# Out projection of a decoder step: seven block products in place of eight

## The chip, the cores and the metric

The kernel runs on one core of a Trainium2 chip. The metric is device microseconds (us) for one execution of the whole program. The kernel before takes 1403.93 us (median of 3 runs, 1402.64 to 1404.23). Its engines are called here as the profile calls them: PE (TensorE: matmuls; PEld are its weight loads), DVE (VectorE), ACT (ScalarE), POOL (GpSimd) and SP (the queue from which nearly all DMA transfers are issued). Each engine works through its own queue in order; semaphores make one wait for another. SBUF is the on-chip memory of 128 partitions, PSUM the small memory into which PE accumulates.

## The reference

One decoder layer runs over 1024 prompt tokens and 64 sample tokens (8 sequences of 8). Of its work the change touches the third line:

```python
branch_a = a_mix @ w_pa ;  branch_b = attn @ w_pb
mixed = sigmoid(g_a) * branch_a + sigmoid(g_b) * branch_b      # 1088 tokens x 1024
h = x + mixed @ w_o                                            # w_o: 1024 x 1024
y = h + relu(rmsnorm(h) @ w_up)**2 @ w_down                    # D_FF = 4096
```

Everything is float32. A few other outputs (pooling state, key/value windows) leave the chip on the side.

## The kernel before, in words

**Layout.** Activations are kept transposed: a row tile is 128 channels (partitions) by tokens. The 1088 tokens (`TOK`) stand in two halves of `H` = 544, called j = 0 and 1. A matrix of 1024 channels is eight row tiles k = 0..7. A float32 factor is split into a high part (an ACT copy to fp32r, L116) and a low part (DVE: source minus high, L117); a product takes three passes, high x high, high x low, low x high (`PASSES`). `split` issues the pair L116, L117. Split weights lie in one large tile, `places`; split activations in `act[0]` (high) and `act[1]` (low).

**Stages around the change.** First come the gate products (`pg`), which already use seven block products where eight would be the plain way; then the branch units (`pab`, `ab_unit`), sixteen of them, 36 matmuls each, first the eight of token half 0 and then the eight of half 1 in the row-block order d = 2, 0, 1, 3. A unit loads its two sigmoid gates (`gg0`, `gg1`), and its `post` multiplies them into the two branch products and adds them (DVE, L1643 and L1644); the mixed row is then split into `act`. Next is the out projection (`ph`), a loop over token half j, weight panel d (four panels of 256 output channels) and m = 0, 1 (128 channels each): one output row tile of 544 tokens is two `gemm` calls (264 and 280 tokens), each of 8 k-tiles x 3 passes, so 48 matmuls to a row and 768 in all. Both token halves read the whole of `w_o`, so it is loaded and split twice (32 loads of 256 KB, `raw_o`). After a row's matmuls, DVE adds the input x (L1751 in half 0; L1754 in half 1, where ACT has copied x into place, L1752); the row is stored to DRAM (`h_d`), squared on ACT (L1760) and summed for the norm (L1761). While half 1 is being multiplied, the norm of half 0 is finished: `norm_sums` (a small PE product `rth` at L1708, two DVE rows, a power on POOL), `norm_spread` (a DVE row `dg`, then the PE product `bc`, L1721), the eight `normed` rows on DVE (L1724), and `first_half`, which splits them into `act` and stores them. Last come the up projection (`pz`, seven block products again) and the down projection (`pd`). The sums for the second token half's norm are taken after the first `pz` product.

**What sets the order.** The order of PE's instructions is the order of the program text: PE works through products one after the other. Each queued piece has a `prep` (weights are split, sums formed; issued up to three pieces ahead), an `mm` (its matmuls) and a `post`; `run` steps through them. What ACT, DVE, POOL and SP do is put in order by a scheduler when the program is built, and from then on each of them keeps that order. PSUM holds four accumulator tiles for these products (`xtile`, used in turn), so a product that opens a new tile waits until the tile of four openings earlier has been read. `rr` gives buffers in turn in the same way: a load into a buffer waits for the last reader of what was there. POOL's queue also issues copies of the sample key/value windows to the outputs (`out_kv_sample`).

Of the kernel before, what the change touches and what calls it, by code (L numbers as in the profile page):

```python
# [7 lines left out]
F32 = mybir.dt.float32  # L8
# [7 lines left out]
P = 128  # L16
# [21 lines left out]
def decoder_step(ctx, tc, i, o):  # L38
# [183 lines left out]
    pg_d = dp.tile([8, P, H], F32, name="pg_d")  # L222
    ts_d = dp.tile([4, P, 4, H], F32, name="ts_d")
# [1340 lines left out]
    abs_, abq = right("ab0")  # L1564
    for n in T:
        B[n if n == "22" else f"T{n}"] = version(*T[n])
    abt = [abq.tile([P, 7 * 576 + H], F32R, name="ab0"), None]
    gg_first = {(m, x): abq.tile([P, H], F32, name=f"ggf{m}{x}") for m in range(2) for x in range(2)}

# [27 lines left out]
    AB_AT = (3072, 6144, 0, 9216)  # L1597
# [6 lines left out]
    gabs = gab = None  # L1604
    held_back = []

    def turn_to_ab():
        nonlocal gabs, gab
        gls.close()
        gqs.close()  # L1610
        gabs, gab = left("gab")
        abt[1] = gab.tile([P, 7 * 576 + H], F32R, name="ab1")

    def ab_unit(j, d, m):
        g = {}

        def load():
            for x in range(2):
                g[x] = gg_first[m, x] if j + d == 0 else rr(gab, [P, H], F32, name=f"gg{x}_{j}{d}{m}", tag=f"gg{x}", bufs=4)
                behind_pe(dma(g[x], g_d[4 * x + d, m][:, half(j)]))  # L1620
# [20 lines left out]
        def post():  # L1641
            for x in range(2):
                v_.tensor_tensor(two(g[x]), two(g[x]), xs_of(g["x"][x], ab_cut(j, x)), op=ALU.mult)  # L1643
            v_.tensor_tensor(g[0], g[0], g[1], op=ALU.add)  # L1644
            k = 2 * d + m
            out = lambda: split(*(act[s][k][:, half(j)] for s in range(2)), g[0])
# [5 lines left out]
            else:  # L1652
                out()

# [16 lines left out]
    run()  # L1671
    gabs.close()
    abs_.close()
    rows_s.close()


    wq = pool("wq", reuse_waits="tile")
    raws = {}
# [13 lines left out]
    y1s, y1p = right("y1")  # L1692
    nps, np_p = right("hn")
    hqs, hq_p = right("hq")
    y0s, y0p = right("y0")
    fours = [[pool_.tile([P, 4, H], F32, name=f"y{j}_{a}") for a in range(2)] for j, pool_ in enumerate((y0p, y1p))]
    y = [[fours[j][k // 4][:, k % 4] for k in range(KD)] for j in range(2)]
    sqa = [np_p.tile([P, H], F32, name=f"sqa{j}") for j in range(2)]
    hms = np_p.tile([P, 10], F32, name="hms")
    hr = np_p.tile([P, 10], F32, name="hr")  # L1700
    v_.memset(hr, 0.0)
# [28 lines left out]
    todo = []  # L1730
    place[0] += (2 - (place[0] + 8)) % 3
    for j in range(2):
        for d in range(4):
            wt = by_k(panel(i["w_o"][d], f"o{j}{d}"))
            if j == 0:
# [502 lines left out]
```

## Time and profile before

| what | before |
|---|---|
| runs | 1403.93 us median (1402.64 to 1404.23) |
| the profiled execution | 1407.21 us, its span 1405.4 us |
| PE busy | 1394.7 us (99% of the span) |
| DVE busy | 958.3 us (68%) |
| ACT busy | 753.7 us (54%) |
| POOL busy | 255.3 us (18%) |
| gate products end, branch products start | about 547 us |
| out projection (`ph`), first and last matmul | 634.7 to 732.3 us, 768 matmuls |

The profiled execution is 3.3 us above the median of the runs, which is within what single executions differ by, and 1.8 us above its own span. The busy shares are means over stages that have different limits: POOL's 18% lies almost all in the first 400 us, and between the branch products and the up projection it does next to nothing. DVE's 68% is not even either: in the branch products it has stretches with no gap at all. What counts for a change in one stage is which wait ends last in that stage.

### The profile page before, as it was taken

The page shows a single profiled execution, that of the slowest core. Times are in us where ns is not written, and L with a number is a line of the kernel's source. Part 1 is how long each engine was busy: PE and PEld are TensorE (multiplying, and loading weights), DVE is VectorE, ACT ScalarE, POOL GpSimd, SP SyncE. Part 2 cuts the span into 40 slices and gives each one's busy share as a digit, 9 for nine tenths or more (in the row PEclk, how much of TensorE's full clock was granted, in tenths as well). Part 3 has the DMA queues.
Part 4 walks back from the last instruction along what each step waited for, and adds up shares of the span by engine and source line. Part 5 has one row for each costly group of instructions (what it writes and reads, how often), then busy time and mean ns, then how long its engine had stood idle before and what let it go on. Part 6 is the DMA issues. An engine that isn't in the chain of part 4 may idle for free.

```text
span 1405.4 us, 29330 instructions
## 1 busy us (share of the span) xinstructions
PE 1394.7 (99%) x11101; PEld 1344.4 (96%) x11101; DVE 958.3 (68%) x1714; ACT 753.7 (54%) x1778; POOL 255.3 (18%) x362
## 2 busy tenths in 40 slices
PE   9999999999999999999999999999999999999998
PEld 8988987887999999999999999999999999999998
DVE  7778744776776767876468678665665686664566
ACT  8556775787765323563336455454554544444443
POOL 0744355676500000000000000000000000000100
PEclk9999999999999999999999999999999999999999
DMA  6455876755477777975468668856758988787674
GB/s 215 132 178 169 252 234 211 223 137 141 123 255 228 247 233 239 314 237 176 133 200 285 227 221 275 267 195 213 251 191 270 332 275 261 230 245 231 206 257 169
DMA packets 180701, 311.96 MB, mean 222 GB/s; under 512 B 26824, under 2 KB 82574, under 8 KB 178511
## 3 DMA queue, kind: packets, MB, share of 16 engines
q1 hardware_dynamic: 174926, 258.04, 57.0%
q0 software_dynamic: 5632, 52.04, 11.5%
q8 instruction: 87, 1.43, 0.4%
q14 instruction: 56, 0.45, 0.1%
HBM read 239.94 MB, written 122.12 MB: 258 GB/s over the span
## 4 chain that ended last, share of the span: by engine, by line
PE 70%; DMA 2%; DVE 1%; ACT 0%; issue 0%; SPq 0%; DVEq 0%; ACTq 0%
PE pz L1318 23%; PE pd L2096 23%; PE pg L1318 11%; PE ph L200 7%; PE pab L1318 4%; DMA raw_ab<-in_w_ab_dram 1%; DMA raw_d<-in_w_down_dram 0%; ACT places L116 0%; PE pog0b L723 0%; PE sg0b L690 0%; PE tpg0b L709 0%; PE pk L200 0%; PE pv L200 0%; SPq L127 0%; DVE places L117 0%
## 5 line engine op out<-in xcount | busy, mean ns | idle before, releaser
L2096 PE MATMUL pd<-places 128*128 128x272 f32 x2688 | 332.0, 287 | 0.7 <-DVE t L1960 0.7
L2096 PEld LDWEIGHTS pd<-places 128*128 128x128 f32 x2688 | 331.6, 188 | 0.9 <-DVE t L1960 0.9
L116 ACT ACTIVATE places<-raw_d 128x544 fp32r<-128x544 f32 (+1 forms) x176 | 110.5, 646 | 161.9 <-DMA raw_d<-z_d 51.3
L2136 POOL DMA_DIRECT2D out_kv_sample_dram<-in_cache_kv_dram x96 | 47.0, 490 | 793.1 <-ACT places L116 583.9
L117 DVE TENSOR_TENSOR places<-raw_d,places 128x544 fp32r<-128x544 f32 (+1 forms) x176 | 122.5, 711 | 91.7 <-ACT places L116 90.7
L1318 PE MATMUL pz<-act,places 128*128 128x280 f32 (+1 forms) x1080 | 139.4, 287 | 0.0
L1318 PEld LDWEIGHTS pz<-act,places 128*128 128x128 f32 x1080 | 135.9, 188 | 0.0
L200 PE MATMUL ph<-act,places 128*128 128x280 f32 (+1 forms) x768 | 96.6, 287 | 0.0
L200 PEld LDWEIGHTS ph<-act,places 128*128 128x128 f32 x768 | 96.0, 188 | 0.1
L1318 PE MATMUL pg<-act,places 128*128 128x264 f32 (+1 forms) x576 | 75.6, 288 | 0.0
L1318 PEld LDWEIGHTS pg<-act,places 128*128 128x128 f32 x576 | 72.6, 188 | 0.6 <-issue 0.3
L1318 PE MATMUL pz<-places,apart 128*128 128x264 f32 (+1 forms) x528 | 67.9, 287 | 0.0
L1318 PEld LDWEIGHTS pz<-places,apart 128*128 128x128 f32 x528 | 66.6, 188 | 0.0
L200 PE MATMUL pqk<-places,act 128*128 128x512 f32 x240 | 62.2, 410 | 0.0
L1318 PE MATMUL pz<-act,apart 128*128 128x264 f32 (+1 forms) x456 | 59.1, 287 | 0.0
L1318 PEld LDWEIGHTS pz<-act,apart 128*128 128x128 f32 x456 | 57.5, 188 | 0.1
L200 PEld LDWEIGHTS pqk<-places,act 128*128 128x128 f32 x240 | 45.8, 196 | 10.1
L874 POOL TENSOR_TENSOR pck<-pck,qs 128x256 f32<-128x256 f32 x64 | 49.9, 812 | 21.6 <-DMA pck<-own_d 7.6
L652 POOL TENSOR_TENSOR mr<-ms,mhalf 128x4 f32<-128x4 f32 (+2 forms) x39 | 51.3, 1317 | 2.9 <-POOL ms L651 0.2
L329 PE MATMUL a<-act,places 128*128 128x384 f32 (+1 forms) x288 | 50.9, 334 | 1.0 <-ACT act L307 0.9
L1318 PE MATMUL pab<-ab,places 128*128 128x264 f32 (+1 forms) x384 | 50.6, 287 | 0.2 <-DVE gg L1643 0.2
L329 PEld LDWEIGHTS a<-act,places 128*128 128x128 f32 x288 | 47.9, 188 | 2.9 <-ACT act L307 1.8
(436 smaller groups left out, 2811.7 us busy)
## 6 DMA issues: line engine op xcount, KB each, us to landing
out_kv_sample_dram<-in_cache_kv_dram POOLq DMA_DIRECT2D x72, 480.0 KB, 4.8
raw_d<-z_d SPq DMA_DIRECT2D x112, 272.0 KB, 4.3
z_d<-t SPq DMA_DIRECT2D x80, 272.0 KB, 4.0
raw_d<-in_w_down_dram SPq DMA_DIRECT2D x80, 256.0 KB, 3.8
raw_u<-in_w_up_dram SPq DMA_DIRECT2D x64, 256.0 KB, 4.0
raw_qkv<-in_w_in_dram SPq DMA_DIRECT2D x36, 256.0 KB, 3.8
own_d<-in_cache_kv_dram POOLq DMA_DIRECT2D x32, 256.0 KB, 3.4
pck<-own_d SPq DMA_DIRECT2D x16, 512.0 KB, 4.7
```

The lines of the kernel that those rows point to most:

```text
L116: ins = s_.activation(dst_hi, src, AF.Copy)
L117: v_.tensor_tensor(dst_lo, src, dst_hi.bitcast(F32), op=ALU.subtract)
L200: last_mm[0] = t_.matmul(out, lhs(a, k), rhs(b, k), start=(j == 0), stop=(j == len(terms) - 1))
L329: last_mm[0] = t_.matmul(pts[m][:, :n], wt[:, a, kk, m * P:(m + 1) * P], act4[b][kk][:, :, part4(c)], start=(p == 0 and kk == 0), stop=(p ...
L652: last_norm[0] = g_.tensor_tensor(r[:n, :H], ms[:n, :H], mhalf[:n, :H], op=ALU.pow)
L874: ins = g_.tensor_tensor(out, *others, op=ALU.mult)
L1318: last_mm[0] = t_.matmul(out[c], lhs(*term), rhs(*term, c), start=(first and n == 0), stop=(n == len(terms) - 1), skip_group_check=not first)
L2096: last_mm[0] = t_.matmul(outs(chain[t], Q)[c], A[:, a, t * P:(t + 1) * P], Z[:, b, c], start=(fresh and f == 0 and n == 0), stop=(f == NG ...
L2136: ins = g_.dma_start(d, a)
```

## The change

The out projection is rewritten as seven block products. Tokens are cut in two halves (column blocks of the mixed matrix), channels in two halves (k = 0..3 and 4..7), and the output channels of a panel f in two (m = 0, 1), so a panel is a 2 x 2 by 2 x 2 block product. With weight blocks A11, A12, A21, A22 and mixed blocks B11 .. B22, the seven products use sums of weights and sums of mixed rows (`sum1`, `sum2`, `sum3`), and the outputs are sums of products. A block product is 4 k-tiles x 3 passes x 2 column halves = 24 matmuls; four panels by seven products are 28 products or 672 matmuls. They run in the order

- 1 and 2 of panels 0 and 1, then of 2 and 3 (positions 0 to 7; these need only the token half that is finished first),
- 6, 7, 4 of panels 0 and 1 in turn (positions 8 to 13), then of panels 2 and 3 (14 to 19),
- 5 and 3 of panels 0 and 1 (20 to 23), then of panels 2 and 3 (24 to 27).

Beside that:

- The mixed rows of token half 0 are also stored to DRAM (`m_d`, eight stores of 272 KB) and eight times loaded back: into `early`, `gg1_back` and the not yet used half of `y`.
- New sums of mixed rows: sum1 and sum2 on DVE, sum3 and `y[1] -= t2f` on POOL. Their splits go to `places` (t_spot) and to `act`.
- New sums of weights for each panel (`sums_6`): A11 -= A21 and S2 = A22 - A11 on DVE, A21 += A22 and A12 -= S2 on POOL.
- x is added differently: `post2` adds it to one row on DVE (from PSUM) and to three more on POOL (strided reads of x by token). The x tiles are now eight loads of 544 KB into three buffers, where they were four loads of 1088 KB into two. A copy of product 1 out of PSUM is made on ACT.
- POOL so gets 28 tensor_tensor instructions of 128x544 or 128x512 in this place: 4 sum3, 4 `y[1] -= t2f`, 12 in `post2`, 8 sums of weights.
- `w_o` is loaded once, as eight quarters of 256 KB for products 1 and 2 and then as whole panels into the raw buffers (sixteen loads of 256 KB).
- The norm of token half 0 moves: `norm_sums(0)` between the column halves of position 21, `norm_spread(0)` and four `normed` after 22, four more after 23, `first_half` spread over 23 to 26.

The core of the diff:

```diff
+    def sum1(k):
+        b11 = mixed[0, k]
+        v_.tensor_tensor(b11, mixed[1, k], b11, op=ALU.subtract)
+        split(*(act[s][k][:, half(1)] for s in range(2)), b11)
+    def sum3(k):
+        g_.tensor_tensor(mixed[1, k], mixed[1, 4 + k], mixed[1, k], op=ALU.subtract)
+    def sum2(k):
+        t = t2f.setdefault(k, mixed[0, k])
+        v_.tensor_tensor(t, mixed[1, 4 + k], mixed[0, k], op=ALU.subtract)
+        split(*(t_spot(2, k, s) for s in range(2)), t)
...
+    def open_out():
...
+        for k in range(4):
+            dma(y[1][4 + k], m_d[4 + k])
+        for k in (2, 3):
+            sum1(k)
+            sum3(k)
+            sum2(k)
+        for k in range(4):
+            g_.tensor_tensor(y[1][4 + k], y[1][4 + k], t2f[k], op=ALU.subtract)
...
+    def load_x(f, m):
+        xr[f, m] = rr(hq_p, [P, TOK], F32, name=f"xr{f}_{m}", tag="xr", bufs=3)
+        dma(xr[f, m], i["xT"][:, 2 * f + m])
...
+    def put_out(src, key):
+        put_at[0] += 1
+        return put_weights(weights_at(1152 * (put_at[0] % 3)), src, [], key)
+    def load_out(f):
+        raws[f] = [raw_tile(f"o{f}_{a}") for a in range(2)]
+        for n in range(0, 2048, 512):
+            behind_pe(dma(raws[f][n // 1024][:, n % 1024:n % 1024 + 512], i["w_o"][f][:, n:n + 512]))
+    def put_plane(n, src):
+        hi, lo = (act_t[s][:, 4 + n, 8:520].rearrange("p (a b n) -> p a b n", a=2, b=2) for s in range(2))
+        split(hi, lo, src.rearrange("p (a b) n -> p a b n", b=2))
...
+        def post2():
+            v_.tensor_tensor(two(y[0][2 * f]), xs_of(q["x"]), by_token(xr[f, 0], 0), op=ALU.add)
+            out_row(0, 2 * f)
             for m in range(2):
-                kk = 2 * d + m
-                po = xtile(f"ph{kk}_{j}")
...
-                    gemm(outs(po, cut)[c], KD, lambda s, k: wt[:, s, k, m * P:(m + 1) * P],
-                         lambda s, k: act[s][k][:, part(c, cut, j * H)])
+                g_.tensor_tensor(two(y[1][2 * f + m]), two(y[0][2 * f + 1]), by_token(xr[f, m], 1), op=ALU.add)
+            g_.tensor_tensor(two(y[0][2 * f + 1]), two(y[0][2 * f + 1]), by_token(xr[f, 1], 0), op=ALU.add)
...
+        def sums_6():
+            A11, A12, A21, A22 = (quarter(f, m, a) for m in range(2) for a in range(2))
+            S2 = sum_tile(f"o2_{f}")
+            v_.tensor_tensor(A11, A11, A21, op=ALU.subtract)
+            v_.tensor_tensor(by_tile(S2), A22, A11, op=ALU.subtract)
+            g_.tensor_tensor(A21, A21, A22, op=ALU.add)
+            g_.tensor_tensor(A12, A12, by_tile(S2), op=ALU.subtract)
+            return put_out(S2, "T2")
...
+    for products_of in ((1, 2), (6, 7, 4), (5, 3)):
+        for f in (0, 2):
+            for n in products_of:
+                for ff in (f, f + 1):
+                    out_groups[ff](n)
...
+    between_of[5, 1] = lambda once=[lambda: norm_sums(0)]: once and once.pop()()
+    after(22, lambda: load_first(0), lambda: norm_spread(0), lambda: [normed(k, 0) for k in range(4)])
+    after(23, lambda: first_half(0), lambda: first_half(1), lambda: [normed(k, 0) for k in range(4, 8)])
+    after(24, lambda: load_first(1), lambda: first_half(2), lambda: first_half(3))
```

**POOL, from the first copy of x to the weights of position 9.** Before the change POOL had no such rows: between the branch products and `rth` its queue held only window copies. Of the changed kernel, in the names of the program (`y1_0` is `y` of half 1, rows 0 to 3; `y0_1` half 0, rows 4 to 7; `xr2_1` is x for panel 2, m = 1; `raw_o0_1` the second half of panel 0 of `w_o`; `sm_o2_0` the sum S2 of panel 0):

```order
L1863 TENSOR_TENSOR y1_0_8340<-y0_0_8338,xr0_1_8405 128x544
L1758 TENSOR_TENSOR y1_1_8341<-y1_1_8341,gg1_back3_8220 128x544
L1863 TENSOR_TENSOR y1_0_8340<-y0_0_8338,xr1_0_8437 128x544
L1864 TENSOR_TENSOR y0_0_8338<-y0_0_8338,xr0_1_8405 128x544
L1863 TENSOR_TENSOR y1_0_8340<-y0_0_8338,xr1_1_8473 128x544
L1864 TENSOR_TENSOR y0_0_8338<-y0_0_8338,xr1_1_8473 128x544
L1863 TENSOR_TENSOR y1_1_8341<-y0_1_8339,xr2_0_8515 128x544
L1863 TENSOR_TENSOR y1_1_8341<-y0_1_8339,xr2_1_8517 128x544
L1875 TENSOR_TENSOR raw_o0_0_8547<-raw_o0_0_8547,raw_o0_1_8548 128x4x128
L1864 TENSOR_TENSOR y0_1_8339<-y0_1_8339,xr2_1_8517 128x544
L1863 TENSOR_TENSOR y1_1_8341<-y0_1_8339,xr3_0_8589 128x544
L1876 TENSOR_TENSOR raw_o0_1_8548<-raw_o0_1_8548,sm_o2_0_8597 128x4x128
```

One more row stands ahead of these, the first of its kind (`y1_0 <- y0_0, xr0_0`), which reads what ACT copied out of the product at position 0. The last row, A12 -= S2 of panel 0, is the thirteenth.

**ACT, the weights of positions 8 to 11.** Before the change ACT's rows here were splits of `raw_o` in the order in which PE uses them, with a square in between. Of the changed kernel (`sm_o2_0` are the weights of position 8, `sm_o2_1` those of 9; `raw_o0_0` and `raw_o1_0` to `places` those of 10 and 11; the rows to `act0` put A21 and A12 away for positions 20 to 23):

```order
L116 ACTIVATE places_77<-sm_o2_0_8597 128x2x2x128
L116 ACTIVATE act0_71<-raw_o0_0_8547 128x512
L116 ACTIVATE places_77<-raw_o0_0_8547 128x2x2x128
L1822 ACTIVATE hq6_0_8671<-y0_1_8339 128x544
L116 ACTIVATE places_77<-raw_o1_0_8591 128x2x2x128
L116 ACTIVATE act0_71<-raw_o0_1_8548 128x512
L116 ACTIVATE places_77<-sm_o2_1_8638 128x2x2x128
L116 ACTIVATE act0_71<-raw_o1_0_8591 128x512
```

The split for position 9 (`sm_o2_1`) stands behind the split for position 11 (`raw_o1_0` to `places`), which is written to the spot of `places` that position 8 reads, and behind the A12 row of panel 0 (`raw_o0_1`), which reads what POOL's thirteenth row has written.

**DVE, at the norm of the first half.** Of the kernel before (`ph2_1` is the out projection's output row 2 in half 1):

```order
L1717 TENSOR_TENSOR dg0_9001<-cst_58,hr_8292 128x640
L1754 TENSOR_TENSOR y1_0_8287<-ph2_1_8952,y1_0_8287 128x544
L1724 SCALAR_TENSOR_TENSOR y0_0_8285<-y0_0_8285,cols_59,bc0_9002 128x544 x4
L1724 SCALAR_TENSOR_TENSOR y0_1_8286<-y0_1_8286,cols_59,bc0_9002 128x544 x4
L1761 TENSOR_TENSOR sqa1_8290<-sqa1_8290,hq2_1_9008 128x544
L117 TENSOR_TENSOR act1_72<-y0_0_8285,act0_71 128x544 x4
L117 TENSOR_TENSOR act1_72<-y0_1_8286,act0_71 128x544 x2
L1754 TENSOR_TENSOR y1_0_8287<-ph3_1_9011,y1_0_8287 128x544
```

Of the changed kernel (`ph1_9075` is the accumulator tile of panel 1, read here after position 23; `ph0_9047` that of panel 0):

```order
L1798 TENSOR_TENSOR dg0_9149<-cst_58,hr_8345 128x640
L1823 TENSOR_TENSOR sqa1_8343<-sqa1_8343,hq3_1_9112 128x544
L1857 TENSOR_TENSOR y1_0_8340<-y1_0_8340,ph0_9047 128x544
L1805 SCALAR_TENSOR_TENSOR y0_0_8338<-y0_0_8338,cols_59,bc0_9150 128x544 x4
L1805 SCALAR_TENSOR_TENSOR y0_1_8339<-y0_1_8339,cols_59,bc0_9150 128x544 x4
L1823 TENSOR_TENSOR sqa1_8343<-sqa1_8343,hq0_1_9143 128x544
L117 TENSOR_TENSOR act1_72<-y0_0_8338,act0_71 128x544
L117 TENSOR_TENSOR places_77<-raw_uf0_9146,places_77 128x4x128
L117 TENSOR_TENSOR act1_72<-y0_0_8338,act0_71 128x544
L1857 TENSOR_TENSOR y1_0_8340<-y1_0_8340,ph1_9075 128x544
```

In both, all eight `normed` rows stand ahead of the next reading of a `ph` tile; in the changed kernel two sums of squares, two activation splits and a weight split stand there too, and the tile that is read is the one that the product at position 25 opens anew.

More of the change, by code (lines that the diff above doesn't have):

```diff
@@ L1770, in decoder_step @@
+    after(24, lambda: load_first(1), lambda: first_half(2), lambda: first_half(3))
+    after(25, lambda: (load_first(2), load_first(3)), lambda: first_half(4), lambda: first_half(5))
+    after(26, lambda: first_half(6), lambda: first_half(7))
+    run()
     y0s.close()
```

199 lines of the change are left out of this document (140 added, 59 removed).

## The prediction

> **What bounds the kernel now.** I read the page's busy shares first, then the chain of work that ended last, then the waits and the busy time by stretches around the branch products and the out projection.
>
> ```profile
> PE 1394.7 (99%) x11101; PEld 1344.4 (96%) x11101; DVE 958.3 (68%) x1714; ACT 753.7 (54%) x1778; POOL 255.3 (18%) x362
> ```
>
> PE has nearly no gap, so a matmul less is time saved unless a gap takes its place. The chain, in order of time (start, length, work), shows the stage:
>
> ```profile
> 416.34 131.12 PE pg L1318 x1056
> ...
> 585.20 49.62 PE pab L1318 x396
> 634.82 59.90 PE ph L200 x480
> 694.72 0.94 PE rth L1708 x10
> 695.65 6.18 PE ph L200 x48
> 701.83 0.92 PE bc L1721 x4
> 702.75 29.87 PE ph L200 x240
> ```
>
> The out projection takes 59.90 + 6.18 + 29.87 = 95.95 us for 768 matmuls, 124.9 ns each, with PE never waiting; the gate products, already in seven-product form, take 131.12/1056 = 124.2 ns. The other engines have room here. Columns below: the stretch and its length, then PE, PEld, DVE, ACT and POOL busy, granted clock, DMA share, GB/s.
>
> ```profile
> 590.00:605.00 15.00, 15.00 (x123) 15.00 (x122) 13.94 (x24) 8.45 (x14) 0.00 (x0) 1.00 0.95 299
> ...
> 620.00:634.70 14.70, 14.70 (x120) 14.70 (x119) 10.97 (x18) 7.61 (x14) 0.00 (x0) 1.00 0.54 175
> 634.70:660.00 25.30, 25.30 (x205) 25.30 (x205) 14.54 (x21) 10.02 (x16) 0.00 (x0) 1.00 0.48 161
> 660.00:680.00 20.00, 20.00 (x163) 20.00 (x162) 10.99 (x15) 8.20 (x12) 0.00 (x0) 1.00 0.62 199
> ```
>
> DVE is busy 55 to 57% in the first 45 us of the out projection, POOL not at all. So the question is not whether PE has less to do, but whether four queues can feed it sums, splits and loads at one product each 3 us (24 x 124.5 ns = 2.99).
>
> **The matmuls.** 672 in place of 768: at 124.2 to 124.9 ns they take 83.5 to 83.9 us, a gain of 12.0 to 12.5; I take **-12.2 us**. Whatever PE waits has to stay under this.
>
> **Prices.** From groups of equal instructions between 545 and 760 us (mean ns of one, then idle time before):
>
> ```profile
> L117 DVE TENSOR_TENSOR places<-raw_o,places 128x512 fp32r<-128x512 f32 x32 | 21.4, 688 | 24.1 <-ACT places L116 18.2 <-PE ph L200 5.9
> L1644 DVE TENSOR_TENSOR gg<-gg,gg 128x544 f32<-128x544 f32 x14 | 10.1, 718 | 0.2
> L1751 DVE TENSOR_TENSOR y<-ph,xr 128x544 f32<-128x544 f32 x8 | 9.0, 1120 | 1.6 <-PE ph L200 1.6
> L1754 DVE TENSOR_TENSOR y<-ph,y 128x544 f32<-128x544 f32 x8 | 5.8, 722 | 7.8 <-PE ph L200 7.8
> L116 ACT ACTIVATE places<-raw_o 128x512 fp32r<-128x512 f32 x32 | 19.0, 627 | 15.1 <-DMA raw_o<-in_w_o_dram 9.0 <-PE ph L200 5.4 <-PE pab L1318 0.7
> L1760 ACT ACTIVATE hq<-y 128x544 f32<-128x544 f32 x14 | 9.2, 659 | 34.1 <-DVE y L1754 20.4 <-DVE y L1751 13.7
> L1752 ACT COPY y<-xr 128x544 f32<-128x544 f32 x8 | 8.9, 1167 | 7.8 <-DMA xr<-in_xT_dram 7.8
> L1883 ACT COPY t_e<-pz 128x544 f32<-128x544 f32 x2 | 1.2, 596 | 0.0
> ```
>
> Back to back a DVE row follows the last by 0.65 us (timeline below). For POOL at 128x544 no row exists. The nearest are, on this engine alone, min/median/max in ns:
>
> ```profile
> L301 POOL TENSOR_TENSOR xs<-xs,xs x9: 1840/2146/2317, 32.5 to 52.4; 128x768 f32<-128x768 f32 x6, 128x640 f32<-128x640 f32 x3
> L874 POOL TENSOR_TENSOR pck<-pck,qs x64: 726/742/1362, 180.7 to 285.9; 128x256 f32<-128x256 f32 x64
> L874 POOL TENSOR_TENSOR pcv<-pcv,sc x64: 611/617/1064, 291.7 to 378.0; 128x256 f32<-128x256 f32 x64
> ```
>
> Interpolated between 256 elements (0.61 to 0.74) and 768 (1.84) a row of 544 is 1.3 us. Ten of the thirteen rows discussed below read x by token; the two strided rows above, L1751 against L1754 and L1752 against L1760, cost 1.55 and 1.77 times the plain ones, so such a POOL row lies between 1.3 and 2.3. I take 1.6.
>
> **What POOL does to DVE.** The one place where both worked hard is 32.5 to 49.1 us. There and just before stands the same split, L117 at 128x512 (busy time and count):
>
> ```profile
> 10.00:32.00 22.00, 2.73 (x4) 1.00 0.59 216
> 32.50:49.10 16.60, 12.26 (x6) 1.00 0.37 103
> ```
>
> 0.68 us each without POOL, 2.04 beside it. The timelines of the two engines:
>
> ```profile
> 32.49 16.70 POOL L301 TENSOR_TENSOR xs<-xs,xs 128x768 f32<-128x768 f32 x8 [32.04 <-ACT xs L299]
> 34.43 4.63 DVE L117 TENSOR_TENSOR places<-raw_a,places 128x512 fp32r<-128x512 f32 x2 [2.55 <-ACT places L116]
> ```
>
> Two DVE rows take 4.63 us while POOL rows follow each other: each DVE row waits out a POOL row and takes its 0.65, a pitch of 2.3. I read it as exclusion: of a DVE row with two inputs in SBUF and a POOL row only one runs. With POOL rows of 1.3 a pair costs 1.9. [...]
>
> **The front (positions 8 and 9).** With T = 0 at the first product, position 9 is due at 9 x 3.0 = 27. Its weights stand on ACT behind the A12 row of panel 0, which reads POOL's thirteenth row of the chain shown above. That chain starts with the product at position 0 (ends at 3.0) and its ACT copy (0.6): 3.6 at the earliest; the copy stands behind the split of the last branch row, five DVE rows after that unit's last matmul and with POOL's rows between them, so I take 8. Thirteen pairs at 1.9 make 24.7, then two ACT rows, 1.3: 34.0, **7 us late**. Two things lengthen it. SP issues the store of `post2`'s row ahead of `xr1_1`; the product it belongs to ends at 9, its DVE row comes behind some ten others, near 15, and POOL's sixth row has x only after the load:
>
> ```profile
> xr<-in_xT_dram SPq DMA_DIRECT2D x4, 1088.0 KB, 7.7
> h_d<-y SPq DMA_DIRECT2D x16, 272.0 KB, 4.0
> raw_o<-in_w_o_dram SPq DMA_DIRECT2D x32, 256.0 KB, 3.2
> ```
>
> At 4 to 6 us for 544 KB that is 20 against 17.5 without the wait: +3. And ten strided rows at 1.6 are +3; the loads of panels 0 and 1 behind `xr2` and `xr3`, which wait for POOL to free their buffers, I put at +2. **Front: 15 us.** Bounds: without exclusion the chain is 3.6 + 13 x 1.3 + 1.3 = 21.8 and not late; what stays is that `raw_o0` is issued after POOL's fifth row (10 us) behind 1088 KB of x, so 2.1 MB at 300 GB/s and two DVE rows, 10 + 7.2 + 1.4, plus landing, about 25 to 26 against 24, and that position 9's split comes third behind one that has to wait for position 8's end (3 x 0.63 = 1.9): together 5. With rows of 2.3 it is 15 + 7 = 22.
>
> **The middle (10 to 21).** DVE has one weight split, one output row and a part of a sum per product, and each panel pair four POOL rows: I take **1 us**, from 0 to 4.
>
> **The tail.** The timeline of DVE at the norm before:
>
> ```profile
> 702.79 5.62 DVE L1724 SCALAR_TENSOR_TENSOR y<-y,cols,bc 128x544 f32<-128x544 f32 x8 [0.20 <-PE bc L1721]
> 708.33 0.72 DVE L1761 TENSOR_TENSOR sqa<-sqa,hq 128x544 f32<-128x544 f32 x1
> 708.96 3.90 DVE L117 TENSOR_TENSOR act<-y,act 128x544 fp32r<-128x544 f32 x6
> 712.78 0.72 DVE L1754 TENSOR_TENSOR y<-ph,y 128x544 f32<-128x544 f32 x1
> ```
>
> The reading of a finished tile came 10 us after `bc`, and PE did not mind: a row then took 6 us and four tiles were free. Now position 25 opens the tile that DVE frees behind eight normed rows (5.6), four other rows (2.6) and its own (0.7), so 9.1 after `bc`, that is 10.0 after position 22's end with `bc`'s 0.92. It is due 0.92 + 2 x 3.0 = 6.9 after it: **3 us late**. DVE's rows from `bc` to the sums for the second norm, some 33 at 0.65 to 0.7, are 22 us or more against some 19 of PE (six products and `bc`), of which the 3 us above are already counted; I put that norm 1 us later, and the first one's sums, behind ACT squares, at no more: tail **4 us** (2 to 6).
>
> **DMA.** Eight stores and four of the eight reloads of 272 KB, 3.3 MB, fall on the branch products, whose DMA is at 0.95 in the row of 590; 2.2 MB of x loads leave it. The rest lies where the share is 0.54 and less. I cost it at nothing, up to 3 us if a gate's load slips; PE's only wait there was
>
> ```profile
> PE pab L1318 <- DVE gg L1643: 0.2, 1, 0.2
> ```
>
> **Sum.** -12.2 + 15 + 1 + 4 = +7.8 us. On the profiled execution, 1407.2 us with 1405.4 in its span, 1415.0. That execution lies 3.3 above the median of the runs, so on their scale **1411.7, I say 1412**. With the bounds of front, middle and tail (7 to 22, 0 to 4, 2 to 6) the forecast's own range is 1401 to 1424, and where the exclusion holds most likely 1407 to 1420. Differences under 0.2% (2.8 us) can't be told from none here.
>
> **Rivals.**
> (1) *Hardly any exclusion; faster.* POOL's sums then run beside DVE's. For it speaks a place where the two met and DVE lost nothing:
>
> ```profile
> 245.83 3.44 POOL L874 TENSOR_TENSOR pck<-pck,qs 128x256 f32<-128x256 f32 x4 [1.05 <-issue]
> 247.94 0.40 DVE L1155 TENSOR_TENSOR kw<-qk,wrow 128x256 f32<-128x256 f32 x1
> 248.26 0.41 DVE L1036 TENSOR_TENSOR od<-od,cst 128x256 f32<-128x256 f32 x1
> ```
>
> Against it: the 2.04 us rows, and that POOL's four rows lost 3.44 - 4 x 0.74 = 0.5 here, about the two DVE rows. Front 5, tail 4: -12.2 + 9 = -3.2, **1400.7**; if DVE also has the normed rows out of the way in time, 1398.
> (2) *Exclusion, but DVE goes first and slack takes half of it.* As in these three rows, POOL waits and DVE keeps its pace; DVE works while PE waits. Front 8, tail 4: about 0, **1404**.
> [...]
> That 96 matmuls aren't saved is no rival: PE's queue has 672.
>
> **Chances.** Forecast 0.50; (1) 0.28; (2) 0.12; (3) 0.10. So faster 0.28, the same 0.12, slower 0.60. The range of 8 in 10 runs from the first rival's time to the forecast's upper bound: 1399.5 to 1422.
>
> **What would show it.** In the changed profile: `ph` rows of 124 to 125 ns, 672 of them. PE waits at positions 8 and 9 (the rows of `sm_o2`), 10 us or more together, ended by ACT `places`, and behind it POOL rows L1875, L1876 or loads of `raw_o`. DVE's L117 at 128x512 or 544 near 1.2 to 1.9 us beside POOL rows, and POOL rows above 1.3; L1863 apart from L1758 gives the price of striding. A PE wait of about 3 us before the third of the last products, ended by DVE L1857. Wrong would be: L117 at 0.69 throughout the stage (then rival 1), waits spread evenly over many products (then DVE as a whole is the bound), or a wait in the branch products ended by a DMA.

## The result, and the profile after

The changed kernel takes **1422.91 us** (median of 4 runs, 1417.06 to 1424.57) against 1403.62 for the kernel before (4 runs): a ratio of 1.0135, 95% interval 1.0119 to 1.0152. It is 19.3 us slower where the prediction's sum said 7.8, and just above the upper end of its range.

The page's busy line of the changed kernel:

```profile
PE 1391.8 (98%) x11005; PEld 1339.6 (94%) x11005; DVE 999.5 (70%) x1746; ACT 752.5 (53%) x1782; POOL 303.8 (21%) x390
```

PE has its 96 matmuls less and is busy only 2.9 us less: the matmuls that stayed became slower. The span went from 1405.4 to 1422.8 us, +17.4, and the out projection accounts for it: from its first matmul to its last 634.1 to 749.7, before 634.7 to 732.5. PE's timeline there (start, length, work, and in brackets the wait ahead and what ended it; positions in the order of the products are 0 and 1 in the first row, then 2 to 4 and the first third of 5, the rest of 5 with 6 and 7, then 8 in two rows, 9 with 10 and 11 in two):

```profile
634.05 6.11 PE L1319 MATMUL ph<-act,places 128*128 128x264 f32 x48
640.89 10.14 PE L1319 MATMUL ph<-act,places 128*128 128x264 f32 x80 [0.73 <-ACT y L1891]
653.52 9.77 PE L1319 MATMUL ph<-act,places 128*128 128x264 f32 x64 [2.49 <-DVE places L117]
668.72 2.13 PE L1319 MATMUL ph<-places 128*128 128x264 f32 x8 [5.42 <-ACT places L116]
672.19 4.05 PE L1319 MATMUL ph<-places 128*128 128x264 f32 x16 [1.34 <-DVE places L117]
679.48 2.13 PE L1319 MATMUL ph<-places 128*128 128x264 f32 x8 [3.25 <-ACT places L116]
683.35 10.45 PE L1319 MATMUL ph<-places 128*128 128x264 f32 x64 [1.74 <-DVE places L117]
...
739.15 10.73 PE L1319 MATMUL ph<-act,places 128*128 128x264 f32 x72 [2.97 <-DVE y L1857]
```

The waits in the front add up to 0.73 + 2.49 + 5.42 + 1.34 + 3.25 + 1.74 = **15.0 us**, the later ones to 0.8 in the middle and 3.4 in the tail (2.97, and 0.44 before the second norm): 19.2 in all, where the prediction summed 15, 1 and 4. What it had not summed stands in the lengths of the rows: eight matmuls take 2.13 us in place of 1.0, twenty-four 6.2 in place of 3.0. The busy time by stretches of 2 us (stretch, length, PE busy, granted clock, DMA share, GB/s) shows why:

```profile
652.00:654.00 2.00, 0.48 (x4) 1.00 0.33 126
654.00:656.00 2.00, 2.00 (x12) 0.52 0.93 285
656.00:658.00 2.00, 2.00 (x12) 0.62 1.03 337
...
668.00:670.00 2.00, 1.28 (x6) 0.50 0.89 276
...
686.00:688.00 2.00, 2.00 (x11) 0.50 0.00 0
688.00:690.00 2.00, 2.00 (x17) 0.94 0.00 0
```

After the first wait of 2.49 us the granted clock is a half for about 3.4 us, after the wait of 5.42 for 20.5, after the one at 739 for 3.4 again. Against 3.0 us for 24 matmuls the slow pieces lose 1.8, 3.2, 1.1, 2.4 and 1.7 us: 10.2. The account closes: -12.2 (matmuls) + 19.2 (waits) + 10.2 (slow matmuls) = +17.2, measured +17.4.

The other side of the waits, DVE and POOL, equal instructions in groups (busy time, mean ns; DVE between 640 and 692 us):

```profile
L117 DVE TENSOR_TENSOR places<-raw_o,places 128x512 fp32r<-128x512 f32 x9 | 8.3, 919 | 0.0
L117 DVE TENSOR_TENSOR act<-y,act 128x544 fp32r<-128x544 f32 x4 | 5.6, 1436 | 0.6 <-ACT act L116 0.6
L1823 DVE TENSOR_TENSOR sqa<-sqa,hq 128x544 f32<-128x544 f32 x3 | 4.8, 1614 | 0.2
L1860 DVE TENSOR_TENSOR y<-ph,xr 128x544 f32<-128x544 f32 x4 | 4.5, 1132 | 0.0
...
L1857 DVE TENSOR_TENSOR y<-y,ph 128x544 f32<-128x544 f32 x3 | 2.2, 717 | 5.0 <-PE ph L1319 5.0
```

```profile
L1863 POOL TENSOR_TENSOR y<-y,xr 128x544 f32<-128x544 f32 x8 | 15.8, 1980 | 4.9 <-DMA xr<-in_xT_dram 4.2 <-DVE act L117 0.7
L1864 POOL TENSOR_TENSOR y<-y,xr 128x544 f32<-128x544 f32 x4 | 8.2, 2060 | 0.1
L1875 POOL TENSOR_TENSOR raw_o<-raw_o,raw_o 128x512 f32<-128x512 f32 x2 | 3.4, 1677 | 1.3 <-DVE raw_o L1873 1.3
```

DVE rows with both inputs in SBUF, 0.69 to 0.72 us before, take 0.9 to 1.6 on average in these groups, and up to 2.2; those with one input in PSUM (L1857, L1860) take 0.72 and 1.13 as before (L1754 0.72, L1751 1.12), also with a POOL row beside them: L1857 at 678.69 took 0.71 while L1876 ran, L1860 at 666.18 took 1.12 while L1875 did. POOL's plain sums take 1.7 (L1875), its strided ones 2.0.

### The profile page after: what moved, and what is told of

It is laid out like the page before. It is cut to its first block, busy times and chain, and to the rows that moved or that the text cites. A ratio compares the mean times of both kernels' runs of the same rounds, so it can differ in the third digit from the quotient of the medians.

```text
span 1422.8 us, 29267 instructions
## 1 busy us (share of the span) xinstructions
PE 1391.8 (98%) x11005; PEld 1339.6 (94%) x11005; DVE 999.5 (70%) x1746; ACT 752.5 (53%) x1782; POOL 303.8 (21%) x390
## 4 chain that ended last, share of the span: by engine, by line
PE 65%; DVE 5%; DMA 2%; issue 1%; ACT 0%; SPq 0%; DVEq 0%; ACTq 0%
PE pd L2260 23%; PE pz L1319 23%; PE pg L1319 11%; PE ph L1319 3%; PE pab L1319 3%; DVE places L117 1%; DMA raw_o<-in_w_o_dram 1%; DVE act L117 1%; DVE gg L1699 0%; DMA gg<-g_d 0%; DVE sqa L1823 0%; DVE y L1857 0%; DMA raw_uf<-in_w_up_dram 0%; DVE y L1805 0%; DMA ggf<-g_d 0%
## 5 line engine op out<-in xcount | busy, mean ns | idle before, releaser
L1319 PE MATMUL ph<-act,places 128*128 128x264 f32 (+1 forms) x384 | 52.1, 298 | 6.2 <-DVE y L1857 3.0
L1319 PEld LDWEIGHTS ph<-act,places 128*128 128x128 f32 x384 | 51.1, 199 | 6.8 <-issue 3.2
```

The lines of the kernel that those rows point to most:

```text
L1319: last_mm[0] = t_.matmul(out[c], lhs(*term), rhs(*term, c), start=(first and n == 0), stop=(n == len(terms) - 1), skip_group_check=not first)
```

## The experiments

Each run is given as the difference from the median of the kernel before on the same chip in the same hour (behind it the ratio with its 95% interval, which is not formed from these medians and can differ from them by a microsecond). The kernel before runs between 1401.5 and 1403.6 there; the changed kernel itself, timed once more, was 1420.46:

> The change itself, on the chip of the three runs beside it, as their reference: 1419 to 1424 us, with the spread of some us that it showed before.

It came out at **+18.0 us** (1.0123, 1.0096 to 1.0149), with the same waits within 0.5 us and the same slow stretches.

### Whose rows make the wait: moving POOL's sums, and leaving them out

All 28 sums on DVE:

```diff
-                g_.tensor_tensor(two(y[1][2 * f + m]), ...
+                v_.tensor_tensor(two(y[1][2 * f + m]), ...
...
-            g_.tensor_tensor(A21, A21, A22, op=ALU.add)
+            v_.tensor_tensor(A21, A21, A22, op=ALU.add)
```

> All 28 sums that the change gave to POOL are issued on DVE instead, nothing else changed. Theory A (exclusion of POOL and DVE rows, and the chain of POOL rows ahead of position 9, make most of the wait): POOL rows of 1.3 to 2.1 us go, DVE takes them at about 0.69 (plain) and 1.1 us (strided), its other rows fall back to 0.69; DVE's sum stays about the same but the chain is shorter, PE's waits at positions 5, 8 and 9 fall from 15 to 5 us or less and PE keeps its full clock: 1405 to 1413 us. Rival B (DVE has too many rows anyway, exclusion is only how it shows): no faster than the change, 1421 to 1428.

Measured **+10.3 us** (1411.79; 1.0075, 1.006 to 1.009), 7.7 better than the change. In time theory A (rows of POOL and DVE exclude each other) holds; its picture of the waits does not: 12.2 us stay in the front, 10.8 of them at position 8 and 1.4 at position 10, where DVE now has no gap at all, and the clock is at a half for 13.7 us. The wait of 2.97 us in the tail stays, but no slow stretch follows it (taken up below). DVE's busy time in the window from 640 to 676 (columns as in the prediction, PE first):

```profile
640.00:676.00 36.00, 23.83 (x168) 22.96 (x167) 35.82 (x49) 13.91 (x23) 0.00 (x0) 0.81 0.52 174
```

49 rows in 35.8 us, against 39 rows in 44.6 in the change from 640 to 692 (0.73 us a row against 1.14): without POOL beside it DVE does its own work and POOL's in less time than its own alone.

Only the eight sums of weights on DVE (the last two lines of the diff above):

> Only the eight sums of weights go from POOL to DVE; the 20 other POOL rows stay. Theory A: DVE gains 8 x 0.65 = 5 us, POOL loses 8 x 1.6 = 13, the chain ahead of position 9 two of its thirteen rows: 3 to 5 us faster than the change, 1417 to 1420. Rival B: same as the change or slower, 1422 to 1427.

**+18.7 us** (1420.17; 1.0136, 1.0118 to 1.0154): no gain, a miss for theory A. In the profile POOL waits 8.8 us for loads of x (4.2 in the change), and one L1863 row takes 5.93 us; PE's wait at position 8 rose from 5.4 to 7.1. Why the loads came later was not traced.

Only the twelve additions of x on DVE:

> The twelve additions of x go from POOL to DVE, the 16 other sums stay on POOL. Theory A: a POOL row costs DVE at least what the row costs on DVE itself (1.1 us), so the time falls to near that of the run with all sums on DVE (1411.8): 1410 to 1416. If DVE's row count is the bound, 1420 or more.

**+13.4 us** (1416.96; 1.0098, 1.0076 to 1.012), 1 us above the upper edge of what was expected. Here POOL starves: DVE is busy for 56.0 of the 60 us from 618.5, and POOL's remaining rows there are long (mean of two: 4043 ns for a row that takes 1277 at its shortest in the change).

```profile
L1876 POOL TENSOR_TENSOR raw_o<-raw_o,sm_o 128x512 f32<-128x512 f32 x2 | 8.1, 4043 | 4.9 <-DVE sm_o L1874 2.4 <-ACT hq L1822 2.4
```

The twelve additions of x left out:

> Only the twelve additions of x on POOL are left out, with the same four copies on ACT; the 16 other POOL rows stay. Theory A: these are ten of the thirteen rows ahead of position 9 and 24 of POOL's 50 us here; most of the front's wait goes, 1404 to 1412 us. If instead the sums of weights and of mixed rows are what counts: 1416 to 1422.

The kernel that ran under this name was the change once more, without the edit: **+20.0 us** (1422.42; 1.0131, 1.0108 to 1.0155). It tells only how two timings of the change agree. With the edit:

```diff
-            for m in range(2):
-                g_.tensor_tensor(two(y[1][2 * f + m]), two(y[0][2 * f + 1]), by_token(xr[f, m], 1), op=ALU.add)
-            g_.tensor_tensor(two(y[0][2 * f + 1]), two(y[0][2 * f + 1]), by_token(xr[f, 1], 0), op=ALU.add)
+            if f < 2:
+                for m in range(2):
+                    s_.copy(y[1][2 * f + m], y[0][2 * f + 1])
```

> The twelve additions of x on POOL are left out (x is missing in three of four output blocks; four plain copies on ACT stand in), the 16 other POOL rows stay. As expected for the run of this name before: theory A 1404 to 1412 us, since ten of the thirteen rows ahead of position 9 go; if the sums of weights and of mixed rows are what counts, 1416 to 1422.

**+6.8 us** (1410.36; 1.0052, 1.0031 to 1.0072): the x rows, and with them the buffers of x that POOL had to read before they came free, are more than half of the loss. All 28 left out (the sums of weights and of mixed rows too):

> All 28 sums that the change gave to POOL are left out (four plain copies on ACT stand in for rows that would otherwise be unwritten), so sums of weights, sums of rows and x in three of four output blocks are missing. What is left is the change with no POOL row between the branch products and the norm. Theory A (POOL rows and what waits for them are the front's wait): L117 back at 0.69 us, the front's waits down from 15 to 5 us or less, the clock's long slow stretch gone, the tail's 3 us still there: 1400 to 1408 us, the prediction's first rival plus the tail's slow clock. Rival B (DVE's own row count or the loads hold the front): 10 us of waits stay, 1412 to 1418.

**+2.1 us** (1404.61; 1.001, 0.9998 to 1.0022). This run is the floor of the change: all its products, splits, loads and DVE rows, no POOL row, and in POOL's place only four plain copies on ACT. PE's waits:

```profile
PE ph L1319 <- DVE y L1857: 3.4, 2, 3.0
PE ph L1319 <- ACT places L116: 2.0, 1, 2.0
PE ph L1319 <- DVE places L117: 0.9, 1, 0.9
```

2.9 us in the front, the tail's 3.4 unchanged, and two slow stretches of 3.4 us. The prediction's first rival gave this case 3.2 us under the kernel before. By the profile the out projection lasts 96.5 us here against 98.0 (first matmul to the end of the last); by the runs there is no difference from before. The seven products save next to nothing even when the sums are free, because what is left of the waits and the clock eats some 10 of the 12 us.

### What a POOL row costs DVE, with nothing waiting for it

The run without sums leaves two readings open: DVE was held up *by* POOL's rows, or everything was late because it waited *for* their results. So useless POOL rows were put in the places of the sums (26, since two come before the buffer exists), each started by PE's progress, on a buffer that no one reads:

```diff
+        scr.append(sqa[1])
+    def idle_row():
+        if scr:
+            behind_pe(g_.tensor_tensor(scr[-1], scr[-1], scr[-1], op=ALU.subtract))
...
-            g_.tensor_tensor(A21, A21, A22, op=ALU.add)
-            g_.tensor_tensor(A12, A12, by_tile(S2), op=ALU.subtract)
+            idle_row()
+            idle_row()
```

> The kernel without any of the 28 POOL sums, and in the places where they were issued 26 POOL subtractions of 128x544 on a buffer that nobody needs, paced by PE; no instruction waits for their result until long after. Sums of weights, of mixed rows and x in three of four output blocks are missing as before. Theory A (a POOL row that reads SBUF and a two-input DVE row exclude each other): DVE's L117 beside them at 1.2 to 2 us, the waits at positions 5, 8 and 9 come back in part, 6 to 14 us slower than without them, 1410 to 1418. Theory E (what cost time was waiting for POOL's results, not sharing with it): 1403 to 1407, L117 at 0.69.

and the same with a row that only writes and reads nothing from SBUF:

```diff
-            behind_pe(g_.tensor_tensor(scr[-1], scr[-1], scr[-1], op=ALU.subtract))
+            behind_pe(g_.memset(scr[-1], 0.0))
```

> The same with 26 POOL memsets of 128x544, which read nothing from SBUF. Theory A in the form that only reading rows exclude: 1403 to 1407 us and L117 at 0.69 beside them. If any POOL row that uses SBUF holds DVE up: L117 above 0.8 and slower than 1408.

With the subtractions **+9.8 us** (1413.38; 1.0077, 1.006 to 1.0094), with the memsets **-0.9** (1402.73; 1.0001, 0.9988 to 1.0015). One DVE group and POOL's, first with the subtractions (22 of the 26 fall in the 60 us shown), then with the memsets:

```profile
L117 DVE TENSOR_TENSOR act<-y,act 128x544 fp32r<-128x544 f32 x4 | 5.1, 1305 | 0.3 <-ACT act L116 0.3
...
L1643 POOL TENSOR_TENSOR sqa<-sqa 128x544 f32<-128x544 f32 x22 | 31.8, 1447 | 55.1 <-PE pab L1319 49.2 <-PE ph L1319 4.5
```

```profile
L117 DVE TENSOR_TENSOR act<-y,act 128x544 fp32r<-128x544 f32 x4 | 2.7, 721 | 2.4 <-ACT act L116 2.4
...
L1643 POOL MEMSET sqa<- 128x544 f32 x26 | 14.4, 553 | 82.2 <-PE pab L1319 50.4 <-PE ph L1319 30.7
```

So what the prediction read as exclusion is shown by itself: the subtractions, which read SBUF, held two-input DVE rows up (0.72 to 1.31 us) and were held up (their shortest is 1.09, their mean 1.45); the memsets, which only write, did neither (0.55 each; 18 two-input DVE rows ran while a memset did, the longest took 0.73, and the groups with both inputs in SBUF stand at 0.69 to 0.72 there). Nothing waits for the subtractions, and they cost 8 to 11 us (9.8 less the 2.1 of the run without POOL rows, or against the memsets). The rest of the change's 18, some 8 us, is then left to the sums' results arriving late and to strided rows being longer; those two were not told apart. (The loads of `w_o` are part of the first: see position 8 below.)

### ACT's order, and fillers ahead of positions 8 and 9

```diff
+        if put_at[0] == 12:
+            behind_pe(marks[-1], put_marks[10])
```

> Only the order on ACT is changed: the weight split of position 11 comes behind that of position 9, so that position 9's split no longer waits behind one that needs position 8's end. The prediction gave this order 1.9 us. Theory A (position 9's sum S2 is itself late, on DVE behind POOL rows): within 1 us of the change, 1421 to 1424. Rival C (ACT's order holds position 9): 2 to 3 us faster, 1419 to 1421.

**+18.0 us** (1419.48; 1.0131, 1.0115 to 1.0146), no different from the change's +18.0. The 1.9 us that the prediction gave to ACT's order did not bind: in the change ACT waits there for DVE's sum, not for its own queue (the row of 678.80, quoted below). With that order and fillers that keep PE busy:

```diff
+        for n in range(warm[0]):
+            last_mm[0] = t_.matmul(x[0], act_t[0][:, 4 + n % 4, H:H + P], act_t[0][:, 4 + n % 4, half(1)][:, part(0)], start=True, stop=True)
...
+    for n, count in ((8, 48), (9, 24)):
```

> The kernel with the order of the last run, plus 48 matmuls without use ahead of position 8 and 24 ahead of position 9, which fill PE's two long waits there; they are overwritten by the product that follows. Theory D (PE's granted clock falls to a half after these waits and that costs time of its own): granted clock 1.00 through positions 8 to 11, and 2 to 5 us faster than the run before, 1417 to 1421, though PE does 72 matmuls more. Rival: the slow clock lies under waits for DVE anyway, no difference, or 1 to 2 us slower where the fillers are longer than the waits.

**+16.7 us** (1418.21; 1.0124, 1.0099 to 1.0149), 1.3 better than without fillers, which these runs can't tell from nothing. In the profile the long slow stretch is gone (two of 3.4 us are left in the front), and the end of position 11 comes 20.9 us late in place of 23.2. The fillers took away 5.1 of 8.5 us of slow matmuls; of the 3.4 that are left, 1.7 stand in positions 9 to 11 with no wait behind them. So in the front about half of the slow matmuls, some 4 us (2.3 + 1.7, an estimate), were a cost of their own; the rest lay under waits that DVE would have caused anyway.

### The tail

The second four normed rows on DVE are held behind the reading of position 23's tile:

```diff
-    after(23, ..., lambda: [normed(k, 0) for k in range(4, 8)])
+    after(23, ..., lambda: [normed(k, 0, True) for k in range(4, 8)])
```

> Only the second four of the eight normed rows on DVE are held behind the reading of position 23's tile, which position 25 waits for; the rest as in the change. The wait of 2.97 us at position 25 should shrink under 0.5. Theory D (a wait of 2.5 us or more also costs a stretch of half clock of 3.4 us, so 1.7 us): 4 to 5 us faster than the change beside it, and no slow stretch near the norm. Without a cost of the clock: 3 us. If the late normed rows only move the wait to the up projection: 0 to 1 us.

**+22.3 us** (1424.75; 1.0149, 1.0119 to 1.0179), not faster. The wait at position 25 is down to 0.2 us; 1.0 us stands at position 27 and 2.7 before the sums of the second norm:

```profile
PE rth L1789 <- DVE sqa L1827: 2.7, 1, 2.7
PE ph L1319 <- DVE y L1861: 1.2, 2, 1.0
```

After that last wait the clock is at a half for 6.8 us. So the order of the normed rows moved the wait and did not remove it. That the number of DVE's rows between the two norms makes the tail, as the prediction had counted them, fits this; no run took rows away.

### What a wait costs PE's clock

In the kernel before PE has no wait in the out projection. Waits were put there: PE held at seven row starts until useless copies on ACT are done, four of them or two (the row's first matmul waits for the last copy); and, as the measure, 24 useless matmuls in the same places.

```diff
+                if j == 0 and kk:
+                    for n in range(4):
+                        ins = s_.copy(sqa[1], cst[:, :H])
+                        if n == 0:
+                            behind_pe(ins)
+                    gap.append(ins)
```

> The kernel before, with PE held at the start of each of seven of the eight rows of the out projection's first half until four useless copies of 128x544 have run on ACT after the matmul ahead: seven waits of 2.5 to 3.3 us, each followed by 6 us of matmuls. Their own length is 17.5 to 23 us. Theory D (a wait of some 2.5 us in a 3.4 us window halves the clock for the next window, 1.7 us of matmul time): 7 x 1.7 = 12 us on top, 1432 to 1439 us, if every wait falls so that a window is nearly empty, less in the measure that it does not. If a wait must fill a whole window (3.4 us) for the clock to fall: nothing on top, 1420 to 1427.

> The kernel before with 24 useless matmuls at the same seven places in place of the waits: 7 x 24 x 0.1245 = 20.9 us more, 1422 to 1426, and the granted clock at 1.00 throughout. It is the measure of PE time without waits.

> As the first of these, with two copies in place of four: seven waits of 1.3 to 1.9 us, 9 to 13 us in all. Theory D: windows stay half busy and the clock stays up, nothing on top, 1412 to 1417. If the clock falls for waits of this length too: up to 12 us on top, 1420 to 1428.

Four copies: **+40.7 us** (1443.60; 1.0286, 1.0269 to 1.0304), above both ranges, since the waits came out at 3.2 to 4.9 us, 27.6 in all. Fillers: **+20.1** (1423.02; 1.0141, 1.0118 to 1.0164). Two copies: **+25.4** (1428.24; 1.0175, 1.0154 to 1.0196); this run was above its expectations for another reason than the clock alone, since three of its seven waits were longer than meant (3.0, 5.3 and 8.0 us: ACT's useless copies stood behind others that waited). That makes it the more telling, because both kinds stand in one trace. Two rows of 48 matmuls from it:

```profile
660.53 7.73 PE L202 MATMUL ph<-act,places 128*128 128x264 f32 x48 [5.32 <-ACT sqa L1748]
669.73 6.25 PE L202 MATMUL ph<-act,places 128*128 128x264 f32 x48 [1.47 <-ACT sqa L1748]
```

and two from the one with four copies:

```profile
665.05 7.77 PE L202 MATMUL ph<-act,places 128*128 128x264 f32 x48 [3.23 <-ACT sqa L1748]
...
677.68 8.47 PE L202 MATMUL ph<-act,places 128*128 128x264 f32 x48 [4.85 <-ACT sqa L1748]
```

After a wait of 1.47 us a row takes 6.2 us as ever, after 3.0 or more 7.7 to 8.9. The stage as one window, four copies, then fillers, then two copies, and last the kernel before:

```profile
630.20:770.50 140.30, 112.75 (x784) 111.01 (x782) 55.75 (x81) 51.85 (x82) 2.67 (x3) 0.88 0.36 120
```

```profile
628.80:746.80 118.00, 118.00 (x951) 117.81 (x950) 54.66 (x79) 34.85 (x53) 2.11 (x3) 1.00 0.42 143
```

```profile
630.50:756.90 126.40, 104.20 (x784) 102.47 (x783) 56.25 (x81) 43.86 (x69) 2.11 (x3) 0.95 0.39 133
```

```profile
634.70:732.60 97.90, 97.90 (x785) 97.71 (x785) 55.79 (x81) 35.28 (x54) 2.11 (x3) 1.00 0.52 172
```

The same matmuls keep PE busy 112.75 - 97.90 = 14.9 us longer with seven waits of 3.2 us and more, 6.3 longer with three of them and four of 1.5: **2.1 us on average for each long wait, none for a wait of 1.5**, on top of the wait. With four copies the clock was at a half for 3.4 us after four of the waits and for 6.8 after three. Time filled with matmuls cost its own length and no more: 118.00 - 97.90 = 20.1 us for 168 of them, 120 ns each, at a granted clock of 1.00.

The length of a wait alone does not decide. In the change a wait of 2.97 us at position 25 brought the clock down; with all sums on DVE the same wait did not (48 matmuls in 6.39). In the run without sums two short waits, one after the other, did (88 matmuls in 13.12 in place of 11.0):

```profile
725.29 6.39 PE L1319 MATMUL ph<-act,places 128*128 128x264 f32 x48 [2.97 <-DVE y L1857]
```

```profile
658.14 1.25 PE L1319 MATMUL ph<-places 128*128 128x264 f32 x8 [1.96 <-ACT places L116]
660.33 13.12 PE L1319 MATMUL ph<-places 128*128 128x264 f32 x88 [0.95 <-DVE places L117]
```

What the traces share is this. In each, the clock changed at whole multiples of 3.41 us from its first change (in the trace of the change at 654.1, 657.5, 667.7, 688.2, 739.4 and 742.8). If PE's busy time is counted in the pieces of that grid, the clock fell after every piece at full speed with at most 1.5 us of work (44 pieces, all traces together; in the change those with 0.93, 0.00 and 0.45, in the kernel before one with 1.14) and after none with more (130 pieces that were not filled; the least of them in the change has 1.62, in the kernel before 2.69). So a wait of 3 us cost nothing more where it fell across two pieces and left more than 1.5 us of work in each; the 2.97 us with all sums on DVE left 2.1 and 1.8. This was read from the traces; no run was made to place a wait on the grid.

## Why the prediction was wrong

**The direction and most terms held.** Slower by more than the bound had 0.60. The gain of 12.2 is in the account above. The waits summed were 15, 1 and 4; measured 15.0, 0.8 and 3.4. POOL's chain was summed to start 8 us after the first product and to end with the A12 row at 40.7 (8 + 24.7 + 3 + 3 + 2): it started at 642.20 - 634.05 = 8.2 and ended at 39.2.

```profile
642.20 4.19 POOL L1863 TENSOR_TENSOR y<-y,xr 128x544 f32<-128x544 f32 x2
...
671.48 1.79 POOL L1876 TENSOR_TENSOR raw_o<-raw_o,sm_o 128x512 f32<-128x512 f32 x1
```

**The step that failed is the sum's silence on the clock.** The prediction summed waits as if matmuls kept their 124.5 ns, and left the slow clock to the third rival, at 0.10. Measured, the clock was at a half for 3.4 us after a wait of 2.49 us at position 5 already, and the slow matmuls are a term of 10.2 us that the sum had at nothing; the forecast was 9.6 us short of the measured span. Not all of this term is the clock's own cost: some 4 us in the front and 1.7 in the tail are, and the rest of the miss, some 4 us, is the front itself (next paragraph). The rows that the prediction quotes have the clock at 1.00 throughout, but the trace of the kernel before has a fall, long before the out projection (columns of the stretches as above, PE alone):

```profile
102.00:105.40 3.40, 1.12 (x12) 1.00 0.73 299
105.40:108.80 3.40, 3.40 (x9) 0.50 0.36 128
108.80:112.00 3.20, 3.20 (x24) 1.00 0.52 142
```

A wait of 2.27 us, and the next 3.4 us at a half. The granted clock over the whole span, wherever PE had ever waited, would have put a price on such waits.

**The front was also under-summed, and that its waits came out at 15.0 is luck.** Position 11 ended 23.8 us late (683.35 + 10.45, less 634.05 and 36), of which 15.0 are waits and 8.5 slow matmuls; with fillers it was still 20.9 late, 1.7 of it slow matmuls. So the lateness that DVE, POOL and the loads set was about 19, not 15. The step was to end the front's sum at POOL's thirteenth row and two ACT rows. Position 9's weights waited for something else, 5.5 us later: the sum S2 of panel 1 on DVE, behind DVE rows that had themselves been held up, and then for their low split.

```profile
668.02 1.99 DVE L1823 TENSOR_TENSOR sqa<-sqa,hq 128x544 f32<-128x544 f32 x1
...
676.03 2.13 DVE L1823 TENSOR_TENSOR sqa<-sqa,hq 128x544 f32<-128x544 f32 x1
678.09 0.68 DVE L1874 TENSOR_TENSOR sm_o<-raw_o,raw_o 128x512 f32<-128x512 f32 x1
```

```profile
678.80 0.63 ACT L116 ACTIVATE places<-sm_o 128x512 fp32r<-128x512 f32 x1 [2.26 <-DVE sm_o L1874]
```

And 6.8 of the 15 us stand at position 8 (5.42 + 1.34), where the sum had only 2 us for waiting loads. Its weights are the S2 of panel 0, and DVE waited for that panel's load. SP issued it 22 us after the first product (655.97 - 634.05), behind two stores that waited for DVE's L1860; the prediction's lower bound had put the issue at 10.

```profile
655.97 2.83 SPq L1835 DMA_DIRECT2D raw_o<-in_w_o_dram  x4
663.63 1.99 DVE L1873 TENSOR_TENSOR raw_o<-raw_o 128x512 f32<-128x512 f32 x1 [1.60 <-DMA raw_o<-in_w_o_dram]
667.22 0.72 DVE L1874 TENSOR_TENSOR sm_o<-raw_o,raw_o 128x512 f32<-128x512 f32 x1
```

Without any POOL row SP still issued it at 16 us, and 2.9 us of wait were left there. No run moved these loads alone, so what they cost by themselves is not shown.

The exclusion was priced into POOL's queue (1.9 us a pair) and not into DVE's, where a POOL row beside a two-input DVE row made that row late too (0.72 to 1.31 us beside the useless subtractions).

**Point by point.** *Prices:* plain POOL rows were taken at 1.3 and strided ones at 1.6; the shortest of them here are 1.28 (L1876) and 1.60 (L1863), so the prices alone were right and their means of 1.5 to 2.1 are the exclusion. *Exclusion:* that the rows hold each other up is shown, by the idle rows (1.31 and 1.45) against the memsets (0.72 and 0.55); that only one of the two runs at a time stays the prediction's reading. The DVE rows with one input in PSUM were not held up: L1857 took 0.72 and L1860 1.13. *ACT's order, 1.9 us of the lower bound:* did not bind. *Tail:* 3 us late at position 25, measured 2.97; it costs 1.7 more by the clock, and reordering moves it only. *DMA at nothing:* PE waited 0.4 us in the branch products, so there it held; the late load of panel 0 is the wait at position 8. *Rival 1:* without exclusion and results to wait for, 3.2 under the kernel before was forecast; +2.1 (-0.3 to 3.1 by the interval) measured; the clock, at a half for twice 3.4 us (an estimate of 1.7 us lost in each), is part of the difference, and the rest was not traced. *Rival 2* fell. *Rival 3*, that PE's clock falls, was right in that, and its 1424 was the nearest in time to 1422.9, by luck: its 20 us are the upper bounds of front, middle and tail (22, 4 and 6) with nothing for the clock, and the waits were 15.0, 0.8 and 3.4. What the clock cost was 2.1 us on average for each long wait put into the kernel before.

## What to carry to other kernels

Where PE sets the end, count a wait of PE twice: its own length, and the slow matmuls after it. Here they cost 2.1 us on average for each wait of 3.0 us or more in the kernel before, and the clock fell where a wait left little work (1.5 us or less) in one of the 3.41 us pieces described above. In these traces every wait above 3.0 us brought the clock down, between 2.1 and 3.0 it depended on where the wait fell, and single waits below 2.0 never did (two close together, of 1.96 and 0.95, did). Before work is given to an idle POOL, look at what DVE does at that time: here a POOL row that reads SBUF cost a busy DVE about as much as the row costs on DVE itself (49 rows in 35.8 us with the sums, 39 in 44.6 beside them), so a gain was left only where DVE was idle or read PSUM (L1857 kept its 0.72 us, L1860 its 1.13). A form that saves matmuls has to be priced at the queue that makes its sums: with all sums left out this one was equal with the kernel before, so placing the sums elsewhere could not by itself have made it win.

## What the runs showed that was not expected

- The clock fell in steps: apart from the end of the kernel, its slow stretches in these traces are 3.4, 6.8, 10.2, 13.7 and 20.5 us long, multiples of 3.41. Whether it fell went with how much PE worked in such a piece, not with an unbroken wait: in the change it fell after one with 0.93 us of work and stayed up after one with 1.62 and two with 2.4.
- While the clock was at a half, it stayed there through PE's further waits: 20.5 us at a half after one wait of 5.4, with PE busy for 1.7 to 2.4 us of each 3.4, and full speed after a piece without a gap (684.8 to 688.2). Over all traces it came back after pieces with 2.9 us of work or more and after none with 2.7 or less (41 pieces).
- POOL starved in one run: with the additions of x on DVE, which was busy for 56.0 of 60 us, a POOL row that takes 1.28 us at its shortest took 4.0 (mean of two).
- Repeated executions of every kernel here differ by some 2 to 8 us, also the kernel before (1400.3 to 1405.4 over 13 runs), while stages compared inside the traces repeat within 1 us: three profiles of the change give 115.1 to 115.8 us for the out projection. For a stage, the trace was the sharper measure.
